# Loading the last row of one tile in fifteen small DMAs: a temperature softmax

## The chip, the cores and the metric

The kernel runs on one core of a Trainium2 chip. The metric is the device time of one execution in microseconds (us). The span in a profile is about 2 us shorter than the time. Every profile used here is at a granted clock of 1.0. (A run is called slow when it is over 1.5% above the fastest of its kernel.)

## The reference, cut to what matters

```
x: (16, 1024, 512) float32
x_scaled = x / 0.5
exp_x = exp(x_scaled - max(x_scaled, axis=-1))
out = exp_x / sum(exp_x, axis=-1)
```

There are 16384 rows of 512 numbers. 33.55 MB go in and 33.55 MB come out, and each row is independent.

## The kernel before

The rows are cut into eight tiles of 128 partitions x 16 rows x 512 numbers (4 MB). A partition's 16 rows lie next to each other in memory, so each partition of a tile is one run of 32 KB. There are six buffers. Loads are issued by SyncE, stores by ScalarE (ACT). VectorE (DVE) and ScalarE work on blocks of eight rows (the first tile begins with two blocks of four).

```
    data = ctx.enter_context(tc.tile_pool(name="data", bufs=6))
    ...
    def load(c):
        xt = tiles[c] = data.tile([P, G, D], fp32, name="xt")
        for lo, hi in FIRST if c == 0 else [(0, G)]:
            nc.sync.dma_start(out=xt[:, lo:hi, :], in_=xr[c][:, lo:hi, :])
    # shift: max of each row (DVE), times -2; exponentials: exp and sum (ACT)
    # scale_vector / scale_scalar: times 1/sum, six rows on DVE, two on ACT
    def store(i):
        c, b, B = blocks[i]
        if b + B == G:
            nc.scalar.dma_start(out=outr[c], in_=tiles[c])

    for i in range(n + 3):
        if i < n:
            if blocks[i][1] == 0:
                load(blocks[i][0])
            shift(i)
            exponentials(i)
        if 1 <= i <= n:
            scale_vector(i - 1)
        if 2 <= i <= n + 1:
            scale_scalar(i - 2)
        if 3 <= i:
            store(i - 3)
```

The framework orders everything by semaphores. It has eight completion semaphores for the DMAs of SyncE and ScalarE together (the issues in the trace name eight, 100 and 102 to 108), and gives them out in turn. A DMA that gets one again first waits until that semaphore's last user has landed (in the change, the first small DMA gets 100 again, which the first load wrote last at 5.45 us, and goes out at 5.47 us). In this kernel the seventeen DMAs go round about twice, and each such wait is for something that has to be over anyway. The seventh and eighth load also wait for the first and second store, because there are six buffers (the stores landed at 68.85 and 88.19 us, the loads were issued at 68.93 and 88.31 us).

Note the order of the loop: a tile's store comes three blocks after its last block. So on ScalarE it stands behind exponentials of later tiles, and a late load also makes stores late. The sixth tile's store follows the last tile's first block, and the seventh tile's store (the last but one) follows all exponentials of the last tile.

Of the kernel before, what the change touches and what calls it, by code (L numbers as in the profile page):

```python
# [1 line left out]

# [4 lines left out]


@with_exitstack
def kernel(  # L10
    ctx: ExitStack,
    tc: tile.TileContext,
    x: bass.AP,
    out: bass.AP,
):
    nc = tc.nc
    fp32 = mybir.dt.float32
    P = nc.NUM_PARTITIONS
    AX = mybir.AxisListType.X
    EXP = mybir.ActivationFunctionType.Exp  # L20
    COPY = mybir.ActivationFunctionType.Copy
    MAX = mybir.AluOpType.max

    D = x.shape[-1]
    xf = x.flatten_outer_dims()
    of = out.flatten_outer_dims()
    N = xf.shape[0]




    G = 16
    C = N // (P * G)
    assert C * P * G == N
    xr = xf.rearrange("(c p g) d -> c p g d", p=P, g=G)
    outr = of.rearrange("(c p g) d -> c p g d", p=P, g=G)

    FIRST = [(0, 4), (4, 16)]
    BLOCKS_FIRST = [(0, 4), (4, 4), (8, 8)]
    BLOCKS = [(0, 8), (8, 8)]  # L40

    data = ctx.enter_context(tc.tile_pool(name="data", bufs=6))
    stats = ctx.enter_context(tc.tile_pool(name="stats", bufs=6))

    ctx.enter_context(tc.manual_schedule())


    warm = stats.tile([P, 1], fp32, name="warm", bufs=1)
    nc.vector.memset(warm, 0.0)  # L49
    nc.scalar.activation(out=warm, in_=warm, func=EXP)  # L50

    tiles = {}
    blocks = [(c, b, B) for c in range(C) for b, B in (BLOCKS if c else BLOCKS_FIRST)]
    state = {}

    def load(c):
        xt = tiles[c] = data.tile([P, G, D], fp32, name="xt")
        for lo, hi in FIRST if c == 0 else [(0, G)]:
            nc.sync.dma_start(out=xt[:, lo:hi, :], in_=xr[c][:, lo:hi, :])  # L59

    def shift(i):
        c, b, B = blocks[i]
        xb = tiles[c][:, b : b + B, :]
        negmax = stats.tile([P, 8], fp32, name="negmax")
        nc.vector.tensor_reduce(negmax[:, 0:B], xb, axis=AX, op=MAX, negate=True)  # L65
        bias = stats.tile([P, 8], fp32, name="bias")
        nc.vector.tensor_scalar_mul(bias[:, 0:B], negmax[:, 0:B], 2.0)  # L67
        state[i] = (xb, bias)

    def exponentials(i):  # L70
        B = blocks[i][2]
        xb, bias = state[i]
        sums = stats.tile([P, 8], fp32, name="sums")
        for g in range(B):
            nc.scalar.activation(  # L75
                out=xb[:, g, :],
                in_=xb[:, g, :],
                func=EXP,
                bias=bias[:, g : g + 1],
                scale=2.0,  # L80
                accum_out=sums[:, g : g + 1],
            )
        state[i] = (xb, sums)

    def scale_vector(i):
        B = blocks[i][2]
        xb, sums = state[i]
        recip = stats.tile([P, 8], fp32, name="recip")
        nc.vector.reciprocal(recip[:, 0:B], sums[:, 0:B])  # L89
        for g in range(B - B // 4):  # L90
            nc.vector.tensor_scalar_mul(xb[:, g, :], xb[:, g, :], recip[:, g : g + 1])  # L91
        state[i] = (xb, recip)

    def scale_scalar(i):
        B = blocks[i][2]
        xb, recip = state[i]
        for g in range(B - B // 4, B):
            nc.scalar.activation(  # L98
                out=xb[:, g, :], in_=xb[:, g, :], func=COPY, scale=recip[:, g : g + 1]
# [7 lines that stand above are left out]
    n = len(blocks)  # L107
# [14 lines that stand above are left out]
# [1 line left out]
_INS = ['x']  # L123
_OUTS = [((16, 1024, 512), 'float32')]


# [23 lines left out]
```

## Time and profile before

The time is 162.36 us (162.35 to 162.37, two runs).

| What | Before |
|---|---|
| Span | 160.4 us |
| Load queue (q1) and store queue (q10), share of 16 DMA engines | 49.4% and 48.5% |
| VectorE, ScalarE busy | 71%, 70% |
| Seventh and eighth load issued | 68.93 and 88.31 us |
| Last load landed | 115.8 us |
| Last two stores issued | 134.60 and 137.05 us |

The page of the kernel before, cut to its DMA lines. The DMA row is the mean busy share of the 16 DMA engines in 40 slices of the span, in tenths.

```profile
span 160.4 us, 517 instructions
...
DMA  5999999999999999999999999999999999999993
...
q1 hardware_dynamic: 1296, 33.56, 49.4%
q10 hardware_dynamic: 1152, 33.55, 48.5%
```

The DMA engines are full from the first slice to the last. 49.4% and 48.5% make 97.9%: this is what bounds the kernel.

What SyncE's DMA queue waited for before:

```profile
SPq L59 <- DMA out_dram<-xt: 75.1, 2, 56.1
...
SPq L59 <- DMA xt<-in_x_dram: 8.5, 1, 8.5
```

Two waits for stores, before the seventh and eighth load, and one for a load. The timeline of VectorE in the kernel before, at the first block of the last two tiles (start, duration, then in brackets the idle time before it and what ended it):

```profile
96.45 4.42 DVE L65 TENSOR_REDUCE negmax<-xt 128x8 f32<-128x4096 f32 x1 [2.57 <-DMA xt<-in_x_dram]
...
115.80 4.42 DVE L65 TENSOR_REDUCE negmax<-xt 128x8 f32<-128x4096 f32 x1 [4.98 <-DMA xt<-in_x_dram]
```

ScalarE's issues of the third store and of the last store but one:

```profile
72.14 0.34 ACTq L105 DMA_DIRECT2D out_dram<-xt  x1
...
134.60 0.34 ACTq L105 DMA_DIRECT2D out_dram<-xt  x1
```

So the last load lands at 115.8 us. From there the computation of the last tile takes 18.8 us to the issue of the last store but one (134.6 us), while the store queue still has work. That gives a few microseconds of slack, no more: a last load that comes later leaves the store queue empty.

### The profile page before, as it was taken

To read this page: it belongs to the slowest core of one execution; us is meant where nothing else is said; L and a number is where in the kernel's file an instruction comes from. 1 tells how busy PE (TensorE), PEld (TensorE's weight loads), DVE (VectorE), ACT (ScalarE), POOL (GpSimd) and SP (SyncE) were. 2 spreads that over 40 slices of the span, in tenths; PEclk is the share of its full clock that TensorE was granted. 3 is DMA by queue.
4 is the path that set the end of the run, shared out by engine and by line. 5 is a ranking of instruction groups with operands and counts; after the bars stand their busy time and mean duration, and the time that the engine had idled before them with its cause. 6 is when DMAs were issued, how large, how long until landed. Compare 5 with 4: busy or idle time off the path is not lost.

```text
span 160.4 us, 517 instructions
## 1 busy us (share of the span) xinstructions
DVE 114.0 (71%) x148; ACT 113.1 (70%) x290; POOL 0.2 (0%) x4
## 2 busy tenths in 40 slices
DVE  0608999999999999999999949996199946000000
ACT  3072579989999999999999995799709999100000
POOL 0000000000000000000000000000000000000000
DMA  5999999999999999999999999999999999999993
GB/s 190 464 425 490 392 417 490 403 392 507 409 368 417 386 441 474 392 417 474 417 409 476 417 400 490 417 400 458 441 409 441 458 409 433 458 400 425 474 409 155
DMA packets 2451, 67.13 MB, mean 419 GB/s; under 512 B 272, under 2 KB 272, under 8 KB 272
## 3 DMA queue, kind: packets, MB, share of 16 engines
q1 hardware_dynamic: 1296, 33.56, 49.4%
q10 hardware_dynamic: 1152, 33.55, 48.5%
q14 instruction: 3, 0.02, 0.0%
HBM read 33.55 MB, written 33.55 MB: 418 GB/s over the span
## 4 chain that ended last, share of the span: by engine, by line
DMA 43%; DVE 34%; ACT 7%; issue 1%; SPq 0%
DMA xt<-in_x_dram 24%; DVE negmax L65 23%; DMA out_dram<-xt 19%; DVE xt L91 9%; ACT xt L75 5%; ACT xt L98 2%; DVE bias L67 1%; DVE recip L89 0%; SPq L59 0%
## 5 line engine op out<-in xcount | busy, mean ns | idle before, releaser
L75 ACT ACTIVATE xt<-xt,bias 128x512 f32<-128x512 f32 x128 | 90.5, 708 | 23.2 <-DVE bias L67 23.2
L65 DVE TENSOR_REDUCE negmax<-xt 128x8 f32<-128x4096 f32 (+1 forms) x17 | 70.8, 4163 | 16.9 <-DMA xt<-in_x_dram 16.9
L91 DVE TENSOR_SCALAR xt<-xt,recip 128x512 f32<-128x512 f32 x96 | 39.6, 482 | 0.6
L75 ACT ACTIVATION_READ_ACCUMULATOR xt<-xt,bias 128x1 f32 x128 | 23.9, 187 | 0.0
L98 ACT ACTIVATE xt<-xt,recip 128x512 f32<-128x512 f32 x32 | 21.0, 707 | 0.0
L89 DVE RECIPROCAL recip<-sums 128x8 f32<-128x8 f32 (+1 forms) x17 | 3.3, 192 | 3.2 <-ACT xt L75 3.2
L67 DVE TENSOR_SCALAR bias<-negmax 128x8 f32<-128x8 f32 (+1 forms) x17 | 2.9, 171 | 0.6
L50 ACT ACT_TABLE_LOAD x1 | 1.3, 1283 | 0.7 <-PEq L134 0.7
L49 DVE MEMSET warm<- 128x1 f32 x1 | 0.1, 59 | 0.8 <-PEq L134 0.8
L50 ACT ACTIVATE warm<-warm 128x1 f32<-128x1 f32 x1 | 0.2, 203 | 0.0
L134 POOL MEMSET const-bfloat16-1.0<- 128x1 bf16 x1 | 0.1, 102 | 0.0
L134 POOL MEMSET const-uint8-127<- 128x1 uint8 x1 | 0.1, 101 | 0.0
L134 POOL MEMSET const-float32-0.0<- 128x1 f32 x1 | 0.1, 99 | 0.2 <-issue 0.2
L134 POOL MEMSET const-float32-1.0<- 128x1 f32 x1 | 0.1, 98 | 0.0
## 6 DMA issues: line engine op xcount, KB each, us to landing
out_dram<-xt ACTq DMA_DIRECT2D x8, 4096.0 KB, 26.2
xt<-in_x_dram SPq DMA_DIRECT2D x7, 4096.0 KB, 30.3
xt<-in_x_dram SPq DMA_DIRECT2D x1, 3072.0 KB, 11.5
xt<-in_x_dram SPq DMA_DIRECT2D x1, 1024.0 KB, 4.7
```

The costliest lines, as they stand in the source:

```text
L49: nc.vector.memset(warm, 0.0)
L50: nc.scalar.activation(out=warm, in_=warm, func=EXP)
L65: nc.vector.tensor_reduce(negmax[:, 0:B], xb, axis=AX, op=MAX, negate=True)
L67: nc.vector.tensor_scalar_mul(bias[:, 0:B], negmax[:, 0:B], 2.0)
L75: nc.scalar.activation(out=xb[:, g, :], in_=xb[:, g, :], func=EXP, bias=bias[:, g : g + 1], scale=2.0, accum_out=sums[:, g : g + 1],)
L89: nc.vector.reciprocal(recip[:, 0:B], sums[:, 0:B])
L91: nc.vector.tensor_scalar_mul(xb[:, g, :], xb[:, g, :], recip[:, g : g + 1])
L98: nc.scalar.activation(out=xb[:, g, :], in_=xb[:, g, :], func=COPY, scale=recip[:, g : g + 1])
L134: nc = _bacc.Bacc("TRN2", target_bir_lowering=False, num_devices=1)
```

## The change

The intent: let each DMA engine get its own count of small packets. A DMA of k partitions, with k below 16, is meant to run on k engines. Fifteen such DMAs, of 2 to 15 and of 9 partitions, cover the 128 partitions of the last row of the sixth tile. They are meant to leave the engines with very different counts, from fifteen packets of 2 KB down to none. Which engines a DMA uses is an assumption in this.

```
+    SPLIT = 5
...
+        if c == SPLIT:
+            nc.sync.dma_start(out=xt[:, 0 : G - 1, :], in_=xr[c][:, 0 : G - 1, :])
+            p = 0
+            for k in (*range(2, 16), 9):
+                nc.sync.dma_start(
+                    out=xt[p : p + k, G - 1, :], in_=xr[c][p : p + k, G - 1, :]
+                )
+                p += k
+            assert p == P
+            return
```

## The prediction

> **What bounds the kernel now.** The DMA engines. The queue part of the page gives the load queue 49.4% and the store queue 48.5% of sixteen engines' span; by the packet records an engine is busy 156.8 us of the 157.5 from first packet to last. VectorE (71%) and ScalarE (70%) have slack. SyncE's issues: loads 1 to 6 go out by 4.2 us, the seventh at 68.9 us and the eighth at 88.3 us, each after a store has landed. The last load lands at 115.8 us; the last two stores are issued at 134.6 and 137.0 us, some 5 us before the queue would run dry.
>
> **Bytes and packets: small.** Nothing is computed differently. The sixth load keeps 30 of 32 KB per row. Packets of 8, 24 and 32 KB took 309, 912 and 1213 ns, so 37.7 ns per KB plus 8: a 2 KB packet about 83 ns. [...] That moves the end by at most 0.7 us (0.4%).
>
> **Issues and waits: the larger term.** Fifteen more issues on SyncE, 0.43 us each by the issue view: 6.4 us, harmless by themselves. But the trace's seventeen DMAs share eight completion semaphores in turn, and a plain test program of the same framework (nothing of this change) shows that a DMA which reuses one waits for its last user to land. The small DMAs take the semaphores of loads 1 to 6 and the first store, landing at 4.7, 12, 22, 32, 42, 57, 69 and 76 us, and SyncE issues in order. So they trickle out, and the seventh load goes out at 74 to 84 us instead of 68.9. The second store may be held too (57.9 to about 70 us), and a wait there stops ScalarE's sequence.
>
> **Critical path.** While one queue is held the other keeps the engines busy, so most lateness is hidden. It is not hidden when both queues run dry near 70 to 78 us (2 to 4 us), or when the last load lands late: about 123 us instead of 115.8, with some 4 us of slack, exposes 3 to 5 us before the last stores. A hand estimate with two queues sharing the measured rate reproduces the old end within 0.3 us and gives +2 to +8 us, by where the second store falls among the small DMAs. I take +5.
>
> **Predicted: 167.2 us, 8 in 10 between 163.3 and 171.5.** Faster by over 2%: 0.02; within 2%: 0.26; slower by over 2%: 0.72.
>
> **What would show it.** SyncE's waits for xt and out_dram before small issues, the seventh load at 74 us or later; a hole in the DMA row between 68 and 80 us or 125 and 145 us; mean rate near 405 GB/s instead of 419; last load landing after 115.8 us, or a store issued late on ScalarE. VectorE and ScalarE busy times unchanged.
>
> **What would make it wrong.** If no semaphore reuse blocks an issue: 162.0 to 163.2 us, same. If the second or third store waits for a late small DMA, it can exceed 171 us. [...]

(The "at most 0.7 us" is an estimate: fifteen packets of 83 ns on one engine, less eight times 75 ns, by which the sixth load's packets get shorter at 37.7 ns per KB, make 0.65 us. The forecast's sum is +5 us, 167.2 us, taken from the hand estimate of +2 to +8 us, which has the holds and the late loads. The packets' term was given beside it.)

## More of the kernel before

Of q1's 1296 packets 1152 are data (nine loads of 128 partitions) and 144 are semaphore writes, one for each of the 16 engines and each load.

Stretches of the kernel before. The columns are the length of the stretch, the busy time of each engine, the granted clock, the DMA share and GB/s.

```profile
80.00:86.00 6.00, 5.93 (x8) 5.83 (x15) 0.00 (x0) 1.00 1.01 433
128.00:134.00 6.00, 2.75 (x8) 6.00 (x18) 0.00 (x0) 1.00 0.98 421
134.00:140.00 6.00, 2.08 (x6) 3.02 (x5) 0.00 (x0) 1.00 1.01 437
140.00:146.00 6.00, 0.00 (x0) 0.00 (x0) 0.00 (x0) 1.00 1.00 431
146.00:152.00 6.00, 0.00 (x0) 0.00 (x0) 0.00 (x0) 1.00 0.99 426
```

Five stretches of six microseconds that matter later: the DMA share is about 1 in each. (One engine's packets overlap by 3 to 4 ns in the records shown later, so a share can read over 1.)

A tile occupies VectorE for 14.3 us (two blocks of some 7.14 us), so a seventh load more than 14.3 us ahead of the last one is soon enough, and one less far ahead is not. Here it landed 19.4 us ahead.

## The result, and the profile after

The time is 171.56 us (171.44 to 171.67, two runs), 9.2 us more. The ratio is 1.0552 (95% interval 1.0509 to 1.0595). Ratios are of fast runs of the same rounds, so not quite the ratio of the medians that are quoted. 162.36 times the ratio is 171.3, just inside the range; the median itself is 0.06 us above its upper end.

The page after:

```profile
span 169.8 us, 537 instructions
...
DMA  5999999999989999998499898999999588598985
...
q1 hardware_dynamic: 1552, 33.56, 47.4%
q10 hardware_dynamic: 1152, 33.55, 46.3%
```

The DMA row has holes now, one at slice 20 and several at the end. q1 has 256 packets more: 128 small ones, and 128 semaphore writes. 128 is the sum of 2 to 15 and 9. So each small DMA wrote its semaphore as often as it has partitions: a DMA of k partitions ran on k engines. The counts were uneven, too: of the 44 small packets that had started by 82.3 us, two engines had eight each and at least four had none (packet records chained by their starts and ends; the trace does not name the engines).

The same stretches after:

```profile
80.00:86.00 6.00, 4.15 (x2) 2.12 (x6) 0.00 (x0) 1.00 0.56 216
128.00:134.00 6.00, 4.61 (x3) 0.75 (x2) 0.00 (x0) 1.00 1.01 437
134.00:140.00 6.00, 5.96 (x8) 5.99 (x17) 0.00 (x0) 1.00 0.63 268
140.00:146.00 6.00, 3.65 (x9) 5.84 (x15) 0.00 (x0) 1.00 1.01 437
146.00:152.00 6.00, 2.67 (x7) 4.57 (x10) 0.00 (x0) 1.00 0.62 262
```

From the shares: 6 x (1 - 0.56) = 2.6 us of DMA time are lost at 80 to 86 us, and 6 x (0.37 + 0.38) = 4.5 us after 134 us. In addition the packets of an engine took 159.3 us in sum where they had taken 157.0 (packet records). 2.6 + 4.5 + 2.3 = 9.4 us, as much as the span grew (169.8 - 160.4).

What SyncE's queue waited for after, and its timeline from 60 us on (L64 are the small DMAs, L71 the loads of whole tiles):

```profile
SPq L64 <- DMA xt<-in_x_dram: 49.4, 8, 10.0
SPq L64 <- DMA out_dram<-xt: 25.7, 1, 25.7
```

```profile
68.24 15.89 SPq L64 DMA_DIRECT2D xt<-in_x_dram  x10
84.25 1.68 SPq L71 DMA_DIRECT2D xt<-in_x_dram  x2
```

The small DMAs wait nine times for the semaphore's last user, 75 us in all, and the last ten go out between 68.2 and 84.1 us. The last two of the nine waits, until 78.98 and 81.48 us, are for the first two small DMAs themselves: issued at 5.47 and 12.74 us, they stood in the queue behind the sixth load, and the first packet of 2 KB ran only at 75.5 us. The seventh load follows at 84.25 us, not at 68.93. The eighth goes at 84.72, earlier than before (88.31), since the second store has landed by then. VectorE at the first block of the last two tiles, after:

```profile
109.98 4.42 DVE L77 TENSOR_REDUCE negmax<-xt 128x8 f32<-128x4096 f32 x1 [10.48 <-DMA xt<-in_x_dram]
...
129.35 4.42 DVE L77 TENSOR_REDUCE negmax<-xt 128x8 f32<-128x4096 f32 x1 [5.00 <-DMA xt<-in_x_dram]
```

The last load lands 13.6 us later (and 19.4 us after the seventh, so it is the later of the two that counts). ScalarE's timeline after:

```profile
83.50 0.34 ACTq L117 DMA_DIRECT2D out_dram<-xt  x1
83.89 0.72 ACT L87 ACTIVATE xt<-xt,bias 128x512 f32<-128x512 f32 x1 [6.96 <-DMA xt<-in_x_dram]
...
148.15 0.34 ACTq L117 DMA_DIRECT2D out_dram<-xt  x1
150.60 0.34 ACTq L117 DMA_DIRECT2D out_dram<-xt  x1
```

The first two lines show the third store, which went out at 72.1 us before. It now waits for the semaphore of the tenth small DMA, until 83.5 us, and ScalarE stands idle for 7 us behind it. The last store but one comes 18.8 us after the last load (148.15 - 129.35), exactly as before. So the end of the kernel hangs on the last load.

The slack can be read off too. Before, the span ended 25.8 us after the issue of the last store but one, since the store queue still had work. After, it ended 21.7 us after it, and 21.6 to 21.9 us after it in all the runs below that lost 5 us or more. The slack was therefore 4.1 us: that store goes out 13.55 us later (148.15 - 134.60), which less 4.1 us makes the 9.4 us by which the span grew.

### The profile page after: what moved, and what is told of

Read it like the earlier page. It is cut to its first block, busy times and chain, and to the rows that moved or that the text cites. A ratio compares the mean times of both kernels' runs of the same rounds, so it can differ in the third digit from the quotient of the medians.

```text
span 169.8 us, 537 instructions
## 1 busy us (share of the span) xinstructions
DVE 114.1 (67%) x148; ACT 112.8 (66%) x290; POOL 0.2 (0%) x4
## 3 DMA queue, kind: packets, MB, share of 16 engines
q10 hardware_dynamic: 1152, 33.55, 46.3%
## 4 chain that ended last, share of the span: by engine, by line
DVE 49%; DMA 33%; ACT 5%; issue 1%; SPq 0%
DMA xt<-in_x_dram 33%; DVE negmax L77 32%; DVE xt L103 15%; ACT xt L87 3%; ACT xt L110 2%; DVE bias L79 1%; DVE recip L101 1%; SPq L71 0%
```

## The experiments

The first theory (A) was the prediction's: reused semaphores hold SyncE and the third store back. The rivals were the uneven counts (1), and fifteen more DMAs as such (2). Each run below was meant to change one thing. The kernel before was timed in the same rounds: 162.41 us for the first four runs, 162.50 for the rest. Differences are of medians. All results were correct. A load's landing is read from VectorE's wait for it, or else from its semaphore's last write.

| Run | What is special | Time, us | Difference | Ratio, 95% |
|---|---|---|---|---|
| e1_even15 | fifteen DMAs, even on engines | 173.09 | +10.7 | 1.0673, 1.0650 to 1.0696 |
| e2_gpsimd | the fifteen, from GpSimd | 164.69 | +2.3 | 1.0143, 1.0125 to 1.0161 |
| e3_two_skew | two DMAs, very uneven | 174.95 | +12.5 | 1.0775, 1.0709 to 1.0840 |
| e4_one_row | one DMA for the row | 168.44 | +6.0 | 1.0376, 1.0360 to 1.0391 |
| e5_hold_only | load whole, SyncE held to 99 us | 169.31 | +6.8 | 1.0417, 1.0377 to 1.0456 |
| e6_one_row_tile2 | one row, third tile | 162.58 | +0.1 | 1.0001, 0.9972 to 1.0030 |
| e7_halves | two DMAs of 8 rows | 168.72 | +6.2 | 1.0388, 1.0349 to 1.0427 |
| e8_half_partitions | row of 64 partitions apart | 171.47 | +9.0 | 1.0547, 1.0512 to 1.0582 |
| e9_one_row_half_stores | e4 with stores in halves | 164.05 | +1.6 | 1.0096, 1.0079 to 1.0113 |
| e10_half_stores | before with stores in halves | 163.73 | +1.2 | 1.0082, 1.0053 to 1.0111 |
| e11_two_rows | two rows, one DMA each | 168.47 | +6.0 | 1.0366, 1.0349 to 1.0383 |
| e12_hold_short | load whole, SyncE held to 84 us | 167.87 | +5.4 | 1.0340, 1.0303 to 1.0377 |

### e1_even15: as many DMAs, no unevenness

```
-            for k in (*range(2, 16), 9):          # k partitions each
+            Q = D // 4
+            parts = [(16 * j, 0, D) for j in range(5)]
+            parts += [(80, q * Q, q * Q + Q) for q in range(4)]
+            for p in (96, 112):
+                parts += [(p, 0, 2 * Q), (p, 2 * Q, 3 * Q), (p, 3 * Q, D)]
+            for p, lo, hi in parts:                # 16 partitions each
```

> Fifteen small DMAs as in the change, but each of 16 partitions (whole, half or quarter rows), so every DMA engine gets the same packets. The program's waits are the same as in the change. Theory (semaphore reuse holds SyncE and the third store): 170 to 173 us, seventh load issued at 83 to 86 us, as in the change. Rival 1 (uneven count of small packets per engine): 162.4 to 163.5 us. Rival 2 (fifteen more DMAs cost time by themselves): about 171 us.

Measured: 173.09 us; seventh load at 84.62 us, third store at 83.49 us. Unevenness is not needed for the loss. (The run did not keep the number of packets: it has 240 small ones, 15 on every engine, where the change has 128 and at most 15 on one. Its q1 has 1776 packets, 1152 and 144 as before, the 240 small ones and 240 semaphore writes, so each of the fifteen DMAs ran on 16 engines.) The trace of the change says the same: its seventh load's semaphore writes come within 0.6 us (109.4 to 110.0), so the uneven counts had left nothing on that load. Rival 1 falls as an explanation of this change. Theory A and rival 2 stand.

### e2_gpsimd: the same DMAs from another queue

```
-                nc.sync.dma_start(
+                nc.gpsimd.dma_start(
                     out=xt[p : p + k, G - 1, :], in_=xr[c][p : p + k, G - 1, :]
```

> The same fifteen small DMAs of 2 to 15 and 9 partitions, issued by GpSimd, which has its own eight completion semaphores. SyncE and ScalarE wait for nothing new. Theory: 162.0 to 163.5 us, seventh load issued near 69 us, third store near 72 us. Rival 1 (uneven packets) and rival 2 (fifteen more DMAs as such): 168 to 172 us.

Measured: 164.69 us, 1.2 us above what theory A expected and well below the rivals' 168 to 172. The seventh load went at 68.15 us. The fifteen DMAs as such do not cost 9 us. Note two things that changed with the queue: the waits, and the time at which the small packets ran. They were issued between 1.3 and 20.5 us, before any store. (On GpSimd the fifteen DMAs waited for one another seven times, 11.4 us in all, so eight found a semaphore free.) The remaining 2.3 us were not followed up: the engines' packets took 157.9 us in sum (157.0 before), and the rest is open.

### e4_one_row and e3_two_skew: almost no extra DMAs

```
-            for k in (*range(2, 16), 9):
+            for k in (128,):        # e4_one_row
+            for k in (51, 77):      # e3_two_skew
```

> The row in one DMA of 128 partitions: the same 128 packets of 2 KB, eight on each engine, one more DMA. Theory and rivals: 162.2 to 162.8 us; more than 163.5 would say that 2 KB packets or the split of the load cost time by themselves.

> The row in two DMAs of 51 and 77 partitions: [...] a larger unevenness than the change's 15 to 0. The two reuse semaphores that are free by 13 us. Theory: 162.4 to 163.8 us [...]. Rival 1: 171 us or more. Rival 2: about 163.6 us.

Both are misses for theory A and for rival 2. (e3 is what rival 1 had expected, but e4_one_row is even and lost time too.) One extra DMA, whose semaphore is free at 5.5 us, costs 6.0 us; two cost even more than the change. (e3 was unsteady, 174.1 to 179.4 us; two of its four runs are slow by the rule above, and the table uses the two fast ones. Cut from its expectation: an assumption of how its two DMAs spread over the engines, and an estimate from that of what the packets cost.) In e4_one_row the loads were not issued late: the seventh went out at 68.62 us (before: 68.93), and the eighth at 82.14, six microseconds earlier than before. But they landed late. VectorE in e4_one_row, then its stretches:

```profile
106.60 4.42 DVE L77 TENSOR_REDUCE negmax<-xt 128x8 f32<-128x4096 f32 x1 [12.12 <-DMA xt<-in_x_dram]
...
125.94 4.42 DVE L77 TENSOR_REDUCE negmax<-xt 128x8 f32<-128x4096 f32 x1 [4.97 <-DMA xt<-in_x_dram]
```

```profile
80.00:86.00 6.00, 5.93 (x8) 5.83 (x16) 0.00 (x0) 1.00 1.03 441
128.00:134.00 6.00, 5.93 (x10) 3.40 (x9) 0.00 (x0) 1.00 0.36 153
...
140.00:146.00 6.00, 2.75 (x8) 6.00 (x15) 0.00 (x0) 1.00 0.61 262
```

The engines are full at 80 to 86 us, so nothing is lost while the small packets run. The two loads come 10 us late, and the holes appear at the end, where the stores have run out: the sixth tile's store went out at 132.85 us, 6.9 us after the last load (before: 122.70, also 6.9 us after it). What moved? The packet records of one DMA engine in e4_one_row, in order (start in us, duration in ns, queue, bytes). The trace does not name the engine; one engine's records were put together by their starts and ends:

```
 72.284   1138  q1   30720
 73.419   1213  q10  32768
 74.634   1213  q10  32768
 75.843     84  q1    2048
 75.923   1213  q10  32768
 77.133     84  q1    2048
 77.213   1213  q10  32768
 78.422     84  q1    2048
```

(A 4-byte semaphore write of q1 at 74.628 is left out. It took a turn as well: like all 16 such writes of the sixth load, it lies between two store packets. So beside a full store queue each further DMA costs an engine one more turn, and that much of rival 2 is true.) The engine takes one packet from the load queue, then one from the store queue. A packet of 2 KB uses a turn of 84 ns, and the store queue answers with 1213 ns. Eight small packets therefore hand the store queue eight turns of 1.21 us, 9.7 us in all, before the seventh load gets anywhere. (With the turn of the row's own semaphore write, and less 0.6 us because the packets of 30 KB are shorter, an estimate is 10.3 us.) The landings moved by 10.1 us each (106.60 - 96.45 and 125.94 - 115.80). The second store finished early in exchange, and so the eighth load was issued early, without use.

This is theory B: the two queues share by packets, not by bytes. In the records above each turn is one packet, a partition's run of 32, 30 or 2 KB (1213, 1138 or 84 ns). An estimate with such turns and the durations of the trace before gave +6.9 us for e4_one_row and +8.7 us for the change with its waits. A shorter one: loads 10.3 us later, less the slack of 4.1 us, make +6.2 us for e4_one_row. The trace of the change shows the turns as well: on one engine a packet of 2 KB started at 77.33 us, its DMA's semaphore write at 78.62, the next packet of 2 KB at 79.84 and its semaphore write at 81.13, with a store packet of 32 KB between any two. The estimate behind the prediction had let the queues share time evenly whatever their packets, so to it a small row was a small load.

Theory B must also pass e3: where some engines have more small packets than others, their loads should come later. The seventh load's semaphore writes there spread from 94.4 to 117.3 us, where before they came within 2 us. The last store but one went out at 150.4 us, 33.1 us (14.3 + 18.8) after 117.3: here the end hangs on the seventh load. The estimate gave that load 110.6 us and only +7.9 us; the rest of this run's loss was not settled. Of rival 1 so much is true: unevenness costs when it is large. In e3, q1 has 14 semaphore writes more than before (1438 packets, less 128 small ones and 1152, less 144), where the one DMA of e4_one_row has 16 (1440 packets): at least two engines had no small packet. How the 128 packets lay on the others was not read.

Rival C for the next runs: packets of 2 KB, or a split load, are slow in themselves.

### e6_one_row_tile2: the same row where no store is queued

```
-    SPLIT = 5
+    SPLIT = 2
```

> The row in one DMA of 128 partitions as in the run that lost 6 us, but on the third tile, which is loaded before any store is queued. Theory B: the packets take turns from nobody, 162.2 to 163.0 us. Rival C (packets of 2 KB, or a load split in two, are slow by themselves): 167 to 169 us again.

Measured: 162.58 us, ratio 1.0001. The same 128 small packets cost nothing on the third tile, which landed at 32.6 us (32.4 before), ahead of the first store (43.8 us). Rival C falls. What costs is the neighbour in the other queue.

### e7_halves: more packets, none small

```
-        for lo, hi in FIRST if c == 0 else [(0, G)]:
+        for lo, hi in FIRST if c == 0 else [(0, 8), (8, G)] if c == 5 else [(0, G)]:
```

> The sixth tile in two DMAs of eight rows: sixteen packets of 16 KB on each engine where there were eight of 32 KB, so eight more turns, and no small packet. Theory B: eight more turns against stores of 32 KB, last load landing near 124 to 126 us, 167.5 to 169.5 us as with the single row. Rival C: 162.2 to 163.0 us.

Measured: 168.72 us, last load at 125.95 us:

```profile
106.58 4.42 DVE L65 TENSOR_REDUCE negmax<-xt 128x8 f32<-128x4096 f32 x1 [12.23 <-DMA xt<-in_x_dram]
...
125.95 4.42 DVE L65 TENSOR_REDUCE negmax<-xt 128x8 f32<-128x4096 f32 x1 [5.00 <-DMA xt<-in_x_dram]
```

Packets of 16 KB, in two DMAs of 2 MB, cost as much as the row of 2 KB: sixteen packets on each engine where there were eight, against stores of 32 KB. What counts is the number of turns.

### e9_one_row_half_stores and e10_half_stores: shorter turns for the stores

```
-            nc.scalar.dma_start(out=outr[c], in_=tiles[c])
+            for lo in (0, 8):
+                nc.scalar.dma_start(out=outr[c][:, lo : lo + 8, :], in_=tiles[c][:, lo : lo + 8, :])
```

> The single row of the run that lost 6 us, with every store in two DMAs of eight rows, so its packets are 16 KB and a turn costs the load queue 0.6 us instead of 1.2, while every other load packet of 32 KB gains on the stores. Theory B: last load back to about 106 to 112 us, 162.3 to 163.8 us. If the loss came from the 2 KB packets or from one more DMA (rival C) it stays: 167.5 to 169 us.

> The kernel before with its stores in two DMAs of eight rows. Loads get ahead (last load near 106 us by theory B), but the engines were busy throughout and the bytes are the same: 162.0 to 163.5 us, no gain.

Measured: 164.05 us with the small row and 163.73 us without it. Halving the packets of the stores removes the row's loss, up to 0.3 us. VectorE at the last tile, in e9_one_row_half_stores and then in e10_half_stores:

```profile
113.30 4.42 DVE L77 TENSOR_REDUCE negmax<-xt 128x8 f32<-128x4096 f32 x1 [5.04 <-DMA xt<-in_x_dram]
```

```profile
112.53 4.42 DVE L65 TENSOR_REDUCE negmax<-xt 128x8 f32<-128x4096 f32 x1 [4.25 <-DMA xt<-in_x_dram]
```

The last load came at 113.3 us, with the row that had made it 125.9, and at 112.5 us without the row. (By the expectations it should have been 106 to 112 and near 106.) Shorter turns are not the whole reason: with halved stores the seventh load waited for the first store until 72.1 us, and the small packets ran from 68.1 to 73.5 us, so they found little of it to delay. The halved stores themselves cost 1.2 us and gain nothing, as the engines had been full before; both came out 0.2 us above their ranges. No run beat the kernel before.

### e11_two_rows: twice the packets

```
+        for lo, hi in FIRST if c == 0 else [(0, 14), (14, 15), (15, G)] if c == 5 else [(0, G)]:
```

> The last two rows of the sixth tile in one DMA of 128 partitions each: sixteen more packets per engine, even, and nothing held (seventh load near 69 us). Theory B with a hand estimate of turns: the stores run out of work first, so the cost stops growing with the count: last load near 119 us, 168 to 170.5 us. A cost per small packet (rival C) would double the single row's 6 us: about 174 us. If this comes out below the change, the hold on SyncE is needed for the rest of the change's 9.2 us.

Measured: 168.47 us. Twice the small packets cost no more than one row (+6.0 and +6.0).

```profile
111.32 4.42 DVE L65 TENSOR_REDUCE negmax<-xt 128x8 f32<-128x4096 f32 x1 [7.19 <-DMA xt<-in_x_dram]
```

The seventh load landed at 111.3 us, the last at 121.0 us, only 9.7 us behind it (4.19 MB in 9.7 us are 432 GB/s, the rate of the full stretches above, 421 to 441): the stores that were ready had run out, and the loads had the engines alone. The end hangs on the seventh load here: 111.3 + 33.1 = 144.4 us, which is when the last store but one went out. So the cost did not grow from eight small packets on an engine to sixteen, and sixteen even small packets with nothing held do not reach the change's 9.2 us.

### e5_hold_only and e12_hold_short: the wait without the packets

```
+        if c == 5:
+            prev = xt[0:16, 0, 0:128]
+            for j in range(2):                 # 4 in e5_hold_only
+                hop = stats.tile([16, 128], fp32, name=f"hop{j}", bufs=1)
+                nc.sync.dma_start(out=hop, in_=prev)
+                prev = hop
```

> The kernel before, the sixth load whole, but after it SyncE issues a chain of four tiny copies, each of which waits for the one before, so the seventh load goes out near 84 us (as in the change) and not at 69 us. No split row. Theory A (semaphore reuse holds SyncE back): about +7 us, 168 to 171 us, last load landing near 124 us. Theory B (a small packet takes a whole turn from the load queue while stores are queued) gives this kernel nothing: if B were all of it, 162.4 to 163.5 us.

> The hold alone with a chain of two tiny copies, so the seventh load goes out at about 85 us, as in the change; in the longer chain it went out at 99 us. Theory A with a hand estimate: last load near 123 us, +5 to +7 us, 167 to 170 us. If only the longer hold costs time: under 164 us.

e5 missed its design: each copy took some 7 us to land beside the stores (6.8 and 7.3 us for the two of e12_hold_short), and the seventh load went at 99.1 us; 169.31 us. e12 was made for that. SyncE's timeline of e12_hold_short, then VectorE's and one stretch:

```profile
76.89 0.56 SPq L64 DMA_DIRECT2D hop<-xt  x1
83.73 0.51 SPq L64 DMA_DIRECT2D hop<-hop  x1
84.42 1.66 SPq L59 DMA_DIRECT2D xt<-in_x_dram  x2
```

```profile
112.11 4.42 DVE L71 TENSOR_REDUCE negmax<-xt 128x8 f32<-128x4096 f32 x1 [18.13 <-DMA xt<-in_x_dram]
```

```profile
80.00:86.00 6.00, 5.93 (x8) 5.83 (x16) 0.00 (x0) 1.00 0.99 427
```

With the seventh load at 84.42 us, as in the change (84.25), and the sixth load whole, the time is 167.87 us: +5.4 us. (The profile is of the slowest of the four runs, 168.90 us.) The seventh load lands at 112.1 us and the last at 121.8 us, so again the end hangs on the seventh. So theory A holds too: a wait of SyncE without the small row costs more than half of the change's loss. (The second copy's packets and semaphore writes ran just before the seventh load's first packets, at 90.3 us, and may have cost it a turn or two of 1.2 us: an estimate. The third store was not held in this run; it went out at 72.24 us.) At 80 to 86 us the engines stay full here, and in e4_one_row too.

### e8_half_partitions: a dose of four, spoilt

```
+            H = P // 2
+            nc.sync.dma_start(out=xt[0:H, :, :], in_=xr[c][0:H, :, :])
+            nc.sync.dma_start(out=xt[H:P, 0 : G - 1, :], in_=xr[c][H:P, 0 : G - 1, :])
+            nc.sync.dma_start(out=xt[H:P, G - 1, :], in_=xr[c][H:P, G - 1, :])
```

> Only partitions 64 to 127 have their last row of the sixth tile loaded apart. If a DMA of 64 partitions uses all sixteen engines, each engine gets four more packets. Theory B: four more turns, seventh and eighth load 5 us later, about as much as the slack: +1 to +3 us, 163.3 to 165.5 us. Rival C at half the dose: about 165.4 us.

Measured: 171.47 us. This does not test the dose. (That the small DMA would give each engine four packets was an assumption; no figure shows it.) The packets of 30 KB from a DMA of 64 partitions took 1762 ns (median) where those of 128 partitions took 1138; those of 32 KB from the other 64 partitions, too, took about 1900 where 1213 were usual. No run here isolates the cause.

## Why the prediction was right or wrong

**Right: the DMA engines bound the kernel, and the computation does not.** VectorE was busy 114.0 us before and 114.1 after; the DMA row got holes.

**Right: reused semaphores hold SyncE.** The seventh load was foretold for 74 to 84 us and went at 84.25. It was not foreseen that SyncE would also wait for small DMAs that landed late. A wait of SyncE to the same time, without the small row, costs +5.4 us in e12_hold_short. That this is close to the +5 that was said is in part luck: the +5 also held 2 to 4 us for queues run dry, and e12_hold_short has no such hole near 80 us. The holes were foretold for 68 to 80 and 125 to 145 us; they came at 80 to 86 and after 134 us.

**Partly wrong: which store is held.** It was said that the second store might be held. It was not (58.0 us); the third was, from 72.1 to 83.5 us. The prediction had this case under what would make it wrong, a second or third store that waits for a late small DMA, and gave it more than 171 us. So it came.

**Wrong: "That moves the end by at most 0.7 us (0.4%)", of the packets.** This term was mis-sized. It counted the 83 ns of a small packet (84 ns measured) and missed that each takes a whole turn while stores of 1213 ns are queued. Eight on each engine cost +6.0 us (e4_one_row), none where no store is queued (e6_one_row_tile2), and as much with 16 KB as with 2 KB (e7_halves). The hand estimate behind the range let the queues share the rate evenly; with a turn of 84 ns against one of 1213 ns they did not. In the change itself the turns worked mainly through the waits: when the seventh load was issued, 104 of the 128 small packets had started, so few were left to take turns from it, but by taking turns they had landed late and held SyncE and the third store.

**Size.** +5 us were predicted and +9.2 measured, at the upper edge of the range. The two causes do not add up (5.4 + 6.0 = 11.4), as both act by making the last two loads late, and the cost of that is bounded: in e11_two_rows it did not grow. What the change has beyond either is the hole at 80 to 86 us, 2.6 us. Both queues are short of work there: the second store has finished early (81.9 us, before 88.2), the third store and the seventh load are still held. e4_one_row and e12_hold_short have no such hole. In both the second store landed as early (82.0 and 81.9 us), but the third had gone out at 72.3 and 72.2 us. So the hole goes with the two holds together, SyncE's and the third store's; e12_hold_short, without a small row, shows that the early second store needs no small packets. This is argued from the traces: no run holds the third store alone or releases it in the change, and the fifteen DMAs on SyncE always bring their waits (e1_even15, with the same waits, lost 10.7 us). How the 9.2 us divide between turns and waits is therefore left open.

## What to carry to other kernels

When two DMA queues are full, compare the packet sizes of both. Here bandwidth was shared by turns (84 ns for 2 KB against 1213 ns for 32 KB), so splitting the rows of one queue handed time to the other (+6.0 us, e4_one_row), even in large DMAs (two of 2 MB with packets of 16 KB, +6.2 us, e7_halves). Before adding DMAs to a queue, list which completion semaphore each will reuse and when its last user lands, because issues behind it are held in order (here SyncE for 75 us in nine waits). A small extra load was free where the other queue was empty (ratio 1.0001, e6_one_row_tile2); then ask which transfer ends late, and whether the end of the kernel hangs on it, here through stores that stand behind it in ScalarE's order.
